# Sums of squares of the second token half in two views instead of four, their single-column products and the root's rows issued one token tile at a time between other products

## The chip, the cores and the metric

The kernel runs on one core of a Trainium2 chip, in one launch. The metric is the device time of the whole program in microseconds (us). Five engines work side by side, each in its own order, and wait for each other through semaphores: PE (TensorE, matrix products; its weight loads are listed apart as PEld), DVE (VectorE), ACT (ScalarE), POOL (GpSimd) and SP, which issues most DMAs. PE writes its results into PSUM banks, everything else works in SBUF.

## The reference

The reference is a trunk of two layers on 1024 tokens of 1024 values. Layer 0 has a forgetting softmax attention (FoX), layer 1 a gated linear attention (GLA); each is followed by a SwiGLU. Every sub-layer is preceded by an RMS norm that is scaled and shifted by a conditioning vector. Cut to what matters here:

```python
def rms_norm(x, g):
    y = xf * lax.rsqrt(jnp.mean(xf * xf, axis=-1, keepdims=True) + EPS)
    return (y * g).astype(x.dtype)

def modulate(h, shift, scale):
    return h * (1.0 + scale[:, None, :]) + shift[:, None, :]

for i in range(DEPTH):                      # DEPTH = 2
    sh1, sc1, g1, sh2, sc2, g2 = jnp.split(c_act @ ada_w[i] + ada_b[i], 6, axis=-1)
    h = modulate(rms_norm(x, norm1_g[i]), sh1, sc1)
    y = forgetting_attention(h, ...) if i == 0 else gated_linear_attention(h, ...)
    x = x + g1[:, None, :] * y
    h = modulate(rms_norm(x, norm2_g[i]), sh2, sc2)
    x = x + g2[:, None, :] * swiglu(h, ffn_w_in[i], ffn_w_out[i])
return rms_norm(x, final_g)
```

The change concerns three of the norms: the second norm of both layers (ahead of the SwiGLU) and the first norm of layer 1 (ahead of the GLA).

## The kernel before

**Layout.** x is held transposed: eight tiles `xs[k]` of 128 features by 1024 tokens, and all work goes over two halves of 512 tokens (`hf` 0 and 1). Each float32 product is made of three products of rounded parts (`mm3`, lines 240 to 243): high times high, high times low, low times high, accumulated in one PSUM bank. A tile of the output sums over k = 0 to 7, so it is 24 products of 512 columns. High parts are made by ACT, low parts (the remainder) by DVE or POOL.

**The end of a sub-layer.** `last_chunk` (line 1079) runs the output projection, for half 0 and then for half 1, over eight feature tiles m. After each, DVE adds the result to `xs[m]` (line 1074), and `SumSq` (lines 571 to 591) takes over: ACT squares the new tile into a view `v[m]` (line 583), and DVE or POOL adds views together (line 590), v0+v1, v2+v3 and so on, as a tree. For half 0 the whole tree is added, to a single view. For half 1 the tree stops early (`LATE1 = 7`): views 0 to 3 are added into view 0, view 5 into view 4, and views 6 and 7 are left alone. These four views, the roots, are what is handed on. At the very end of the program the squares are summed by another branch, which the change leaves alone.

**The norm.** `rms_cols` (line 526) sums over the features, which lie on the partitions: for each of the 4 token tiles and for each root, the view's 128 tokens are loaded as weights and multiplied by a column of ones, into one column of the PSUM tile `sp` (line 531). DVE scales the sums and adds EPS (line 534), POOL takes the power -1/2 (line 535). `rms_rows` (line 538) then spreads the root over the partitions: four products, one for each token tile, with the identity as the moving operand, fill the PSUM tile `rb` (line 543). Each of these float32 products appears in the trace as two instructions. Behind them DVE multiplies x by `rb` and the modulation, and ACT and DVE (or POOL) split the result into high and low parts: `normed` (line 1175) and `split_t` (lines 1182 and 1183) ahead of a SwiGLU, `norm_half` (lines 549 to 569) ahead of the GLA.

**Ahead of the SwiGLU.** `ffn` (line 1140) calls `rms_rows` for half 1 right after `last_chunk` (line 1199), then `second_half` (lines 1209 to 1220, called at line 1327), which norms and splits half 1 and makes the differences that a Strassen-like scheme needs. The first eight output tiles are plain ones (`plain_tile`, line 1330): three on half 0, then four on half 1, then one more on half 0. The first three give PE something to do while half 1 is normed. The order is tied at line 1352: in the second plain tile, products with k of 2 and more stand behind the last single-column product, and those with k of 6 and more behind the last row of `rb` (`GK = (2, 6)`); the third tile stands behind the rows too.

**Ahead of the GLA.** `norm_mixer` (line 1545) calls `norm_half` at the end of layer 0's SwiGLU, for either half. The GLA begins with value projections of half 0's tokens, `gv_body` (line 1611): 48 products of 256 columns each, for two pairs of token tiles. The first is free, the second is tied behind the single-column products (line 1848), and what follows, `a_body` and the rest, behind the rows of `rb` (line 1850).

**What sets the order.** The program is written in one sequence and a planner, which simulates the engines' time (`schedule_with_timeline_sim=True`), makes of it the order in which each engine gets its instructions. It may issue an instruction ahead of earlier written ones. `tc.issue_after(ins)` holds it to an order on one engine without a semaphore: what is traced within stands behind `ins` on the same engine. On the chip the engines keep the planned order.

## Time and profile before

| | us |
|---|---|
| three runs | 2414.92, 2417.11, 2417.97 |
| median of the runs | 2417.11 |
| profiled execution, from first to last instruction (span) | 2415.5 |
| PE busy | 2373.4 (98%) |
| DVE busy | 1672.9 (69%) |
| POOL busy | 1203.4 (50%) |
| ACT busy | 1191.8 (49%) |

The profiled execution is one of its own beside the three runs; no time is given for it but its span. Its mean granted PE clock over the span is 0.993 of full speed. Positions in the trace are counted from the span's start. The single-column products of the three norms stand at 662 to 672 us (SwiGLU of layer 0), 1313 to 1322 us (GLA) and 1751 to 1761 us (SwiGLU of layer 1). In rows of the timeline, neighbours of one kind are merged and their number stands behind an x; a busy time counts instructions in flight, so an engine can be busy without working at its peak. PSUM and SBUF tiles are named with their buffer numbers left out (`sp_b`, `rb_b`, `ss_s`); `p_b` is a SwiGLU tile's sum, `gv_b` one of the value projection, `o_s` a weight, `B` a normed input.

### The profile page before, as it was taken

The numbers are of one execution on the slowest core, as the hardware profiler recorded it, in microseconds if no ns is written. First come the engines' busy times: TensorE is split into PE (matmuls) and PEld (weight loads), VectorE is DVE, ScalarE is ACT, GpSimd is POOL, SyncE is SP. The second block draws the span as 40 slices with busy tenths as digits, with TensorE's granted clock in tenths as the row PEclk, the third lists the DMA queues.
The fourth block names the chain that finished last, engine by engine and source line by source line (L and its number), as shares of the span: only waits on it lengthen the run. The fifth ranks groups of instructions, "written<-read, shape, count | busy, mean of one in ns | idle before, by whom it ended". The sixth has DMA issues, their size and how long they took to land.

```text
span 2415.5 us, 36053 instructions
## 1 busy us (share of the span) xinstructions
PE 2373.4 (98%) x12342; PEld 2018.3 (84%) x12342; DVE 1672.9 (69%) x2789; ACT 1191.8 (49%) x2288; POOL 1203.4 (50%) x1071
## 2 busy tenths in 40 slices
PE   7999999999999999999999999999999999999998
PEld 6788888878888888888888888898888888888888
DVE  6577677676687877876787545435586767675787
ACT  4665555675544444445324856654343333345325
POOL 4343344432347878853263646662335656653262
PEclk9999999999999999999999999999999999999999
DMA  9233333123335555457665334434325444347664
GB/s 272 72 106 114 100 111 105 62 97 114 127 103 178 184 172 174 155 187 260 228 201 171 89 110 126 135 124 154 114 85 172 164 133 151 133 174 256 232 202 148
DMA packets 329359, 361.88 MB, mean 150 GB/s; under 512 B 24460, under 2 KB 252968, under 8 KB 329176
## 3 DMA queue, kind: packets, MB, share of 16 engines
q1 hardware_dynamic: 328984, 359.57, 45.4%
q8 instruction: 97, 1.59, 0.3%
q14 instruction: 86, 0.70, 0.1%
q10 hardware_dynamic: 192, 0.02, 0.0%
HBM read 269.25 MB, written 90.24 MB: 149 GB/s over the span
## 4 chain that ended last, share of the span: by engine, by line
PE 82%; DVE 5%; DMA 4%; ACT 3%; issue 2%; POOL 2%; SPq 1%; DVEq 0%; POOLq 0%; ACTq 0%
PE p_b L243 16%; PE p_b L241 16%; PE p_b L242 16%; PE o_b L979 2%; PE t_b L965 2%; PE qk_b L241 2%; PE qk_b L243 2%; PE qk_b L242 2%; PE s_b L934 1%; PE s_b L935 1%; PE gr_b L243 1%; PE gr_b L242 1%; PE gr_b L241 1%; PE vps_b L241 1%; PE vps_b L242 1%
## 5 line engine op out<-in xcount | busy, mean ns | idle before, releaser
L164 DVE TENSOR_TENSOR o_s<-xv_s,o_s 128x512 fp32r<-128x512 f32 (+1 forms) x376 | 341.4, 911 | 78.4 <-ACT o_s L163 77.5
L163 ACT CAST o_s<-xv_s 128x512 fp32r<-128x512 f32 (+1 forms) x376 | 217.8, 587 | 320.3 <-PE p_b L243 254.4
L242 PE MATMUL p_b<-B,o_s 128*128 128x512 f32 x608 | 238.1, 392 | 0.0
L243 PE MATMUL p_b<-B,o_s 128*128 128x512 f32 x608 | 237.7, 391 | 0.0
L241 PE MATMUL p_b<-B,o_s 128*128 128x512 f32 x608 | 236.2, 391 | 0.0
L945 POOL TENSOR_SCALAR lp_s<-lp_s,st 128x128 f32<-128x128 f32 (+7 forms) x128 | 98.1, 771 | 265.7 <-DVE st L944 214.7
L708 POOL TENSOR_TENSOR ex_s<-xv_s,xv_s 128x512 f32<-128x512 f32 (+1 forms) x64 | 89.1, 1393 | 261.5 <-DMA xv_s<-in_ffn_w_in_dram 97.1
L241 PE MATMUL p_b<-T,o_s 128*128 128x512 f32 x480 | 186.7, 389 | 0.0
L242 PE MATMUL p_b<-T,o_s 128*128 128x512 f32 x480 | 186.7, 389 | 0.0
L243 PE MATMUL p_b<-T,o_s 128*128 128x512 f32 x480 | 180.7, 389 | 0.0
L243 PEld LDWEIGHTS p_b<-B,o_s 128*128 128x128 f32 x608 | 114.7, 189 | 23.9
L241 PEld LDWEIGHTS p_b<-B,o_s 128*128 128x128 f32 x608 | 114.7, 189 | 23.8
L242 PEld LDWEIGHTS p_b<-B,o_s 128*128 128x128 f32 x608 | 114.7, 189 | 23.7
L943 ACT ACTIVATE lp_s<-lp_s,st 128x128 f32<-128x128 f32 (+7 forms) x128 | 99.3, 777 | 61.1 <-DVE st L939 58.7
L381 POOL TENSOR_TENSOR ad_s<-ad_s,ad_s 128x512 f32<-128x512 f32 x62 | 89.4, 1442 | 54.0 <-ACT ad_s L379 29.6
L163 ACT CAST pt_s<-t_b 128x512 fp32r<-128x512 f32 (+1 forms) x160 | 79.6, 547 | 73.5 <-PE t_b L965 72.8
L710 POOL TENSOR_TENSOR xv_s<-ex_s,xv_s 128x512 f32<-128x512 f32 (+1 forms) x64 | 84.9, 1327 | 57.3 <-DVE o_s L164 55.1
L1319 DVE TENSOR_TENSOR ex_s<-ex_s,p_b 128x512 f32<-128x512 f32 x140 | 94.0, 680 | 27.0 <-PE p_b L243 26.9
L164 DVE TENSOR_TENSOR pt_s<-t_b,pt_s 128x512 fp32r<-128x512 f32 (+1 forms) x160 | 96.8, 631 | 13.2 <-ACT pt_s L163 12.9
L243 PEld LDWEIGHTS p_b<-T,o_s 128*128 128x128 f32 x480 | 90.1, 188 | 18.7
L241 PEld LDWEIGHTS p_b<-T,o_s 128*128 128x128 f32 x480 | 90.1, 188 | 18.7
L242 PEld LDWEIGHTS p_b<-T,o_s 128*128 128x128 f32 x480 | 90.1, 188 | 18.7
(1952 smaller groups left out, 7505.7 us busy)
## 6 DMA issues: line engine op xcount, KB each, us to landing
xv_s<-in_ffn_w_in_dram SPq DMA_DIRECT2D x176, 256.0 KB, 3.0
hid_B<-x SPq DMA_DIRECT2D x70, 512.0 KB, 2.7
ad_s<-in_ada_w_dram SPq DMA_DIRECT2D x384, 64.0 KB, 1.9
hid_T<-x SPq DMA_DIRECT2D x36, 512.0 KB, 2.8
xv_s<-in_ffn_w_out_dram SPq DMA_DIRECT2D x96, 192.0 KB, 4.1
ada_s<-in_ada_w_dram SPq DMA_DIRECT2D x128, 128.0 KB, 2.6
xv_s<-in_ffn_w_out_dram SPq DMA_DIRECT2D x40, 256.0 KB, 2.8
T2o<-hid_T SPq DMA_DIRECT2D x18, 512.0 KB, 9.0
```

The costliest lines, as they stand in the source:

```text
L163: nc.scalar.copy(hi, src)
L164: nc.vector.tensor_sub(lo, src, hi.bitcast(F32))
L241: nc.tensor.matmul(ps, ah, bh, start=start, stop=False)
L242: nc.tensor.matmul(ps, ah, bl, start=False, stop=False)
L243: nc.tensor.matmul(ps, al, bh, start=False, stop=stop)
L381: nc.gpsimd.tensor_add(acc, acc, raw)
L708: nc.gpsimd.tensor_add(s1, a21, a22)
L710: nc.gpsimd.tensor_sub(a11, s1, a11)
L943: nc.scalar.activation(lp, lp, AF.Exp, bias=mcur, scale=-1.0, accum_out=st[:, qi, 2:3])
L945: nc.gpsimd.tensor_scalar(lp, lp, st[:, qi, 3:4], 1.0, op0=ALU.mult, op1=ALU.mult)
L965: nc.tensor.transpose(tp[:, i, :], lps[qi][:, psl(2 * b + jj)], ident)
L1319: nc.vector.tensor_add(d, d if src is None else dest(G, src), ps)
```

## The change

It has four parts.

- `SumSq` for half 1 adds on: after m = 5 DVE adds view 4 into view 0, and after m = 6 view 6 into view 0. The roots are now two, views 0 and 7.
- `mm3` issues its three products through a new function `product`. Where a queue `between` holds pieces of work, `product` takes one from it after each product, ties it behind that product, and ties the next product behind the piece.
- `rms_later` gives the norm as such pieces: the sums of one token tile (four pieces), the root (DVE and POOL), a number of empty pieces, and the rows of one token tile (four pieces). With the last row, what follows from it on the other engines is traced.
- The pieces go, ahead of the SwiGLU, between the products of the second plain tile from k = 2 on (8 empty pieces), and ahead of the GLA between the products of the second value projection (13 empty pieces). The old ties to the sums and rows are gone there, except that `a_body` and the rest of the GLA still stand behind the last row. `second_half` is now traced with the last row instead of ahead of the plain tiles, and the GLA's norm of half 1 within the second value projection.

```diff
+    between, tail = deque(), []
+
+    def product(ps, a, b, start, stop):
+
+        with ExitStack() as es:
+            if tail:
+                es.enter_context(tc.issue_after(tail.pop()))
+            nc.tensor.matmul(ps, a, b, start=start, stop=stop)
+        if between:
+            f = between.popleft()
+            with tc.issue_after(last_of("P")):
+                if f is not None:
+                    f()
+            tail.append(last_of("P"))
+
     def mm3(ps, ah, al, bh, bl, start, stop):
-        nc.tensor.matmul(ps, ah, bh, start=start, stop=False)
-        nc.tensor.matmul(ps, ah, bl, start=False, stop=False)
-        nc.tensor.matmul(ps, al, bh, start=False, stop=stop)
+        product(ps, ah, bh, start, False)
+        product(ps, ah, bl, False, False)
+        product(ps, al, bh, False, stop)
...
-    GK = (2, 6)
+    GK = 2
...
+    def rms_later(ss, nm, psr, then, gap=8):
+
+        at = {}
+
+        def sums(t):
+            if t == 0:
+                at["sp"] = psr([P, 4], F32, f"sp{nm}")
+            for i, q in enumerate(ss):
+                nc.tensor.matmul(at["sp"][:, t:t + 1], q[:, psl(t)], ones, start=i == 0, stop=i == len(ss) - 1)
+
+        def root():
+            rs = at["rs"] = sm.tile([P, 4], F32, tag="rs", name=f"rs{nm}")
+            nc.vector.tensor_scalar(rs, at["sp"], 1.0 / D, EPS, op0=ALU.mult, op1=ALU.add)
+            nc.gpsimd.tensor_tensor(rs, rs, mhalf[:, 0:4], op=ALU.pow)
+
+        def row(t):
+            if t == 0:
+                at["rb"] = psr([P, HALF], F32, f"rb{nm}")
+            nc.tensor.matmul(at["rb"][:, psl(t)], at["rs"][:, t:t + 1].to_broadcast([P, P]), ident,
+                             start=True, stop=True)
+            if t == 3:
+                rb_ins.append(last_of("P"))
+                then(at["rb"])
+
+        return ([lambda t=t: sums(t) for t in range(4)] + [root] + [None] * gap
+                + [lambda t=t: row(t) for t in range(4)])
...
     def norm_half(xs, ss, hs, l, hf, psr, tmp):
 
+        if hf:
+            second_norm.extend(rms_later(ss, f"{l}0{hf}", psr,
+                                         lambda rb: norm_views(rb, xs, hs, l, hf, tmp), 13))
+            return
...
-            self.roots = {0: [self.v[0]], 8: [self.v[0]], 7: [self.v[0], self.v[4], self.v[6], self.v[7]],
+            self.roots = {0: [self.v[0]], 8: [self.v[0]], 7: [self.v[0], self.v[7]],
...
+            if self.late == 7 and m in (5, 6):
+                nc.vector.tensor_add(v[0], v[0], v[4 if m == 5 else 6])
...
-        rb = rms_rows(ss1[0], f"{l}11", psr)
...
-        def second_half():
+        def second_half(rb):
...
-        second_half()
...
-                with ExitStack() as es:
-                    for k_, ins in after:
-                        if k >= k_:
-                            es.enter_context(tc.issue_after(ins))
-                    mm3(ps, w.hi[:, k % 4, :], w.lo[:, k % 4, :], hi(t), lo(t), k == 0, k == 7)
+                if k == GK:
+                    between.extend(small)
+                mm3(ps, w.hi[:, k % 4, :], w.lo[:, k % 4, :], hi(t), lo(t), k == 0, k == 7)
...
-        plain_tile(0, 1, 0, ((GK[0], sp_ins[-1]), (GK[1], rb_ins[-1])))
-        plain_tile(1, 0, 0, ((0, rb_ins[-1]),))
+        plain_tile(0, 1, 0, rms_later(ss1[0], f"{l}11", psr, second_half))
+        plain_tile(1, 0, 0)
...
-    with tc.issue_after(sp_ins[-1]):
-        vt.append(gv_body(0, wv, 1))
+    between.extend(second_norm)
+    vt.append(gv_body(0, wv, 1))
```

More of the change, by code (lines that the diff above doesn't have):

```diff
@@ L545, in rms_rows, with norm_views @@
         return rb
-    first_half = []
+    def rms_later(ss, nm, psr, then, gap=8):
[19 more added lines that the diff above has]
+                + [lambda t=t: row(t) for t in range(4)])
+    first_half, second_norm = [], []
     def norm_half(xs, ss, hs, l, hf, psr, tmp):
+        if hf:
+            second_norm.extend(rms_later(ss, f"{l}0{hf}", psr,
+                                         lambda rb: norm_views(rb, xs, hs, l, hf, tmp), 13))
+            return
         rb = rms_rows(ss, f"{l}0{hf}", psr)
         gates = [(SPM, sp_ins[-1]), (RBM, last_ins())]
+        norm_views(rb, xs, hs, l, hf, tmp)
+        first_half.append(last_of("G"))
+        return gates
+    def norm_views(rb, xs, hs, l, hf, tmp):
         cs = hsl(hf)
@@ L566, in norm_half @@
                 nc.gpsimd.tensor_sub(lo, y, hi.bitcast(F32))
-        if hf == 0:
-            first_half.append(last_of("G"))
-        return gates
     class SumSq:
@@ L1326, in ffn, with plain_tile @@
         gs = [Group(*g) for g in GROUPS]
-        second_half()
         wgs = [[[None, None], [None, None]] for _ in range(2)]
-        def plain_tile(kind, m, hf, after=()):
+        def plain_tile(kind, m, hf, small=()):
             wg = wgs[kind]
@@ L1351, in ffn @@
         plain_tile(0, 0, 0)
-        plain_tile(0, 1, 0, ((GK[0], sp_ins[-1]), (GK[1], rb_ins[-1])))
-        plain_tile(1, 0, 0, ((0, rb_ins[-1]),))
+        plain_tile(0, 1, 0, rms_later(ss1[0], f"{l}11", psr, second_half))
+        plain_tile(1, 0, 0)
+        assert not between
         for kind, m, hf in ((0, 0, 1), (0, 1, 1), (1, 0, 1), (1, 1, 1), (1, 1, 0)):
@@ L1847, in trunk @@
     vt = [gv_body(0, wv, 0)]
-    with tc.issue_after(sp_ins[-1]):
-        vt.append(gv_body(0, wv, 1))
+    between.extend(second_norm)
+    vt.append(gv_body(0, wv, 1))
+    assert not between
     with tc.issue_after(rb_ins[-1]):
```

## The prediction

> **What bounds the kernel now.** I read the page first: its span, its busy shares, and the chain of work that ended last.
>
> ```profile
> span 2415.5 us, 36053 instructions
> PE 2373.4 (98%) x12342; PEld 2018.3 (84%) x12342; DVE 1672.9 (69%) x2789; ACT 1191.8 (49%) x2288; POOL 1203.4 (50%) x1071
> PE 82%; DVE 5%; DMA 4%; ACT 3%; issue 2%; POOL 2%; SPq 1%; DVEq 0%; POOLq 0%; ACTq 0%
> ```
>
> TensorE sets the time: it is busy 98% of the span and carries 82% of the chain. Whatever it issues costs time, whatever it skips saves time, and work on the other engines is free until a product waits for it. The change touches three places: the norm of the second token half before the first SwiGLU (site 1, about 669 us), before the GLA mixer (site 2, about 1319 us), and before the second SwiGLU (site 3, about 1758 us). Next, TensorE's timeline at site 1. Columns: start, length, then the instruction; sp are the single-column sums of squares, rb the rows of the root, xN the merged instructions.
>
> ```profile
> 646.22 0.39 PE L243 MATMUL fo1421p_b<-ohh,wo_256l_s 128*128 128x512 f32 x1
> 646.45 0.95 PE L531 MATMUL sp_b<-ones,ss_s 128*128 128x1 f32 x8
> ...
> 649.89 0.39 PE L243 MATMUL fo1431p_b<-ohh,wo_256l_s 128*128 128x512 f32 x1
> 650.12 1.05 PE L543 MATMUL rb_b<-ident,rs 128*128 128x128 f32 x8
> 650.93 0.48 PE L241 MATMUL fo1441p_b<-ohh,wo_512h_s 128*128 128x512 f32 x1
> ...
> 661.93 0.62 PE L241 MATMUL p_b<-B,o_s 128*128 128x512 f32 x2
> 662.38 0.28 PE L531 MATMUL sp_b<-ones,ss_s 128*128 128x1 f32 x2
> ...
> 663.07 0.39 PE L241 MATMUL p_b<-B,o_s 128*128 128x512 f32 x1
> ...
> 668.75 0.39 PE L243 MATMUL p_b<-B,o_s 128*128 128x512 f32 x1
> 668.98 3.40 PE L531 MATMUL sp_b<-ones,ss_s 128*128 128x1 f32 x30
> 672.24 0.48 PE L241 MATMUL p_b<-B,o_s 128*128 128x512 f32 x1
> 672.55 0.40 PE L242 MATMUL p_b<-B,o_s 128*128 128x512 f32 x1
> ...
> 676.11 0.63 PE L243 MATMUL p_b<-B,o_s 128*128 128x512 f32 x1
> 676.53 1.19 PE L543 MATMUL rb_b<-ident,rs 128*128 128x128 f32 x8
> 677.48 0.48 PE L241 MATMUL p_b<-B,o_s 128*128 128x512 f32 x1
> ```
>
> Two things are to be seen. An undisturbed product takes 0.227 us (663.07 to 668.75 is 25 of them). And after the run of 30 single-column instructions the products become slow: rows grow from 0.39 to 0.63 us. The busy time by stretch, with the granted clock (the third number from the end), says why; the stretches are cut where the clock changes:
>
> ```profile
> 666.57:669.98 3.41, 3.41 (x22) 2.98 (x21) 1.31 (x3) 3.11 (x4) 2.63 (x2) 1.00 0.92 350
> 669.98:673.39 3.41, 3.41 (x27) 3.24 (x27) 0.16 (x1) 0.00 (x0) 1.12 (x2) 1.00 0.04 14
> 673.39:676.81 3.42, 3.42 (x11) 2.64 (x10) 0.00 (x0) 0.00 (x0) 0.29 (x1) 0.50 0.00 0
> 1321.93:1325.34 3.41, 3.41 (x18) 3.41 (x18) 0.16 (x1) 0.22 (x1) 1.02 (x1) 0.50 1.22 306
> 1762.24:1765.66 3.42, 3.42 (x10) 2.67 (x9) 0.00 (x0) 0.00 (x0) 0.34 (x1) 0.50 0.00 0
> 1393.60:1403.84 10.24, 9.75 (x35) 8.50 (x34) 4.64 (x9) 6.12 (x12) 6.58 (x7) 0.50 0.51 154
> ```
>
> At each of the three sites the clock falls to half for 3.41 us just after the single-column run, though TensorE counts as busy all through. The stretch that precedes the drop at site 1 (669.98 to 673.39) holds 2.26 us of single-column work and 1.15 us of products, 34%; the one before it, with 2.41 us of products, 71%, brought no drop.
>
> **The change part by part.**
>
> *Half the single-column products.* At each site, 4 token tiles times 4 views are 16 products, which the trace shows as 32 instructions (30 and 2 above). With two views they are 8 products, 16 instructions. Before: 668.75 to 672.55 holds two ordinary products and the 30, so 3.80 - 0.45 = 3.35 us; the early pair costs 661.93 to 663.07, 1.14 us less four products (0.91), 0.23 us. Together 3.58 us, 0.112 each. After, groups of four stand between products. Their price is not in the trace, but its neighbours are: a pair at 0.117 each, and eight at 0.119 each (646.22 to 649.89, 3.67 us, less 12 products, 2.72). It hardly depends on the grouping, so 16 x 0.119 = 1.90 us, and the saving is 1.7 us a site, **5.1 us** for three (bounds 4.9 and 5.4, by 0.12 and 0.112).
>
> *The rows of the root, likewise.* Still 8 instructions; eight together cost 649.89 to 650.93 less a product, 0.81 us. In four pairs at the pair's price it is 0.94. I take +0.1 a site, +0.3 in all (0 to 0.4).
>
> *The clock.* From 672.55 to 676.11 are ten products in 3.56 us, 1.29 too many; from 676.11 over the rows to 677.48 is 1.37 us against 1.04 for the same at 649.89 to 650.93. So one drop costs 1.6 us; three cost 4.8. In the new order four groups of 0.48 and four products of 0.227 last 2.83 us. The emptiest 3.41 us then hold 0.91 + 0.58 = 1.49 us of products, 44%. That lies between the 34% that dropped and the 71% that did not, and nearer to 34%, but with 0.34 us more of products than in the stretch that fell. I take no drop at sites 1 and 3 (bounds: none of the gain, or all of it).
>
> The page "TensorE: Matmul & The Clock Gate" of the Trainium skill (Part 1) says that the half clock follows an idle window of about 3.4 us and that the window runs free. Its length agrees with the 3.41 us here; "idle" does not, since the stretch that led to the drop held 1.15 us of products. By the page's rule alone no window here would be idle in the new order, and the gain would be the whole 4.8 us.
>
> The drops start at 673.39, 1321.93 and 1762.24 us: the distances are 190.0 and 319.0 times 3.4133 us. So the stretches stand on a fixed grid which has no tie to the work, and in other executions a run of 3.26 us will lie otherwise on it. If a drop needs the 2.26 us that preceded this one, it comes at (3.26 + 3.41 - 2 x 2.26) / 3.41 = 63% of the positions. The profiled execution had all three; the runs should have about two. I credit 0.65 x 1.6 = 1.0 us at each of sites 1 and 3.
>
> *The two added additions.* They run on DVE, whose cost is nothing as long as it has idle time, but the first group now waits for the last of them, and with it everything behind it on TensorE. DVE, ACT and POOL at site 1 and both engines at site 2:
>
> ```profile
> 662.81 0.63 ACT L583 ACTIVATE ss_s<-x 128x512 f32<-128x512 f32 x1 [2.62 <-DVE x L1074]
> 666.54 0.74 DVE L1074 SCALAR_TENSOR_TENSOR x<-fo1471p_b,modc,x 128x512 f32<-128x512 f32 x1
> 667.20 0.68 DVE L590 TENSOR_TENSOR ss_s<-ss_s 128x512 f32<-128x512 f32 x1
> 672.42 0.16 DVE L534 TENSOR_SCALAR rs<-sp_b 128x4 f32<-128x4 f32 x1 [4.54 <-PE sp_b L531]
> 672.66 1.02 POOL L535 TENSOR_TENSOR rs<-rs,mhalf 128x4 f32<-128x4 f32 x1 [2.29 <-DVE rs L534]
> 677.76 5.35 DVE L1175 SCALAR_TENSOR_TENSOR yb_s<-x,amul,rb_b 128x512 f32<-128x512 f32 x8 [5.18 <-PE rb_b L543]
> 683.04 2.57 DVE L1183 SCALAR_TENSOR_TENSOR B<-yb_s,modc,B 128x512 fp32r<-128x512 f32 x3
> ...
> 1317.96 0.67 DVE L590 TENSOR_TENSOR se_s<-se_s 128x512 f32<-128x512 f32 x1
> ```
>
> ```profile
> 1318.07 0.28 PE L243 MATMUL gv_b<-wv_4h_s,h1l 128*128 128x256 f32 x1
> 1318.68 3.63 PE L531 MATMUL sp_b<-ones,se_s 128*128 128x1 f32 x30 [0.33 <-DVE se_s L590]
> ...
> 1392.15 0.39 PE L241 MATMUL go_b<-gvt_s,ahl_s 128*128 128x256 f32 x1 [1.97 <-ACT ahl_s L163]
> ```
>
> At site 1 the present last addition ends at 667.88; in a queue such operations follow each other every 0.6 to 0.68 us, so two more end at about 669.1 to 669.2. TensorE comes to the first group at 668.98 - 0.23 (early pair gone) + 0.23 (one product) = 668.98. The wait is 0.2 us and something for a weight load that cannot be pulled ahead: **+0.3 us** each at sites 1 and 3 (bounds 0, if an addition is done before the last column of x, and 1.3, if both come after and are slowed). At site 2 DVE is already late: its addition ends at 1318.63 and TensorE starts 0.05 us later, 0.5 us after its last product should have let it. Two more additions put the start at 1319.9 if both come last, at 1318.7 if they are done before. I take the middle, **+0.7 us** more than now (bounds 0 and 1.3). A wait of 1.2 us and then 2.4 us of thin work (256-column products take half the time) is long enough to halve the clock at some positions of the grid, so of the clock's gain I credit site 2 with half as much, 0.5 us.
>
> *The root and what it feeds.* Between the last sum and the first row the present order needs 672.24 to 673.68 for DVE and POOL, 1.44 us. The new one leaves 10 products at site 1 (2.27 us) and 15 of 0.12 us at site 2 (1.8): covered. From the rows to the first product that needs the second half's weights there are now 30 products, 6.8 us; after the change one product of that tile and 24 of the next, 5.7 us. DVE's first remainder (L1183) is there 683.04 + 0.74 - 677.48 = 6.3 us after the rows. Three products on the high parts alone need no remainder (0.7 us), so it just holds; I put 0 and, if the planner sends a remainder first, 0.6 us a site. Nothing is moved past a DMA queue: the stores of x at both norms stay where they are written, and the added edges tie TensorE's instructions alone.
>
> *Sum.* On the profiled execution: -5.1 (columns) + 0.3 (rows) - 4.8 + 0.8 (clock, site 2 half kept) + 0.3 + 0.3 + 0.7 (waits) = -7.5 us, span 2408.0. The page gives no time for that execution beside its span of 2415.5 us; the runs' median is 1.6 us above it, and the lowest of the three 0.6 us below. For the runs, where the drops are not always there: -5.1 + 0.3 - 2.5 + 1.3 = -6.0, from the median of 2417.1 (2414.9 to 2418.0) to **2411.1 us**.
>
> **The rivals.**
>
> *The clock falls all the same* (0.15). Products between groups fill 44%, nearer to the 34% that fell. For it: TensorE counted as busy in both stretches, so the drop follows something finer than that. Against it: the share is higher by 0.34 us of products. Then -5.1 + 0.3 + 1.3 = -3.5, 2413.6 us.
>
> *The planner gives it back* (0.17). All engines' orders behind the sites are worked out anew. The trace has an example of what such an order can cost: 1.97 us of waiting at 1392.15, and the 10.24 us at half clock that follow. Where such a wait arises new, half of 10.24 us less what TensorE waited through, about 4, and 2 are lost: 6, which eats the gain, 2417 us. That the products go on without a gap at sites 1 and 3 speaks against it there. The same mechanism the other way (0.08), this wait gone: 2405 us.
>
> *The first group blocks TensorE* (0.10): the slower case. The trace shows an addition that the planner leaves lying: the square of 662.81 is ready at 663.44, its addition starts at 667.20, 3.8 us later, behind other work of DVE. If the last addition, whose square is ready at 667.35, is left as long, the first group starts after 671.8, 2.8 us late; TensorE is in order, so the tile behind it waits as well. An idle stretch of 2.8 us also halves the clock as before, and the waits pay nothing back: three sites cost 8.4, less 5.1, plus 0.3 and about one drop more than now, 1.6: +5.2, 2422 us. It decides from 1.6 us of wait a site. Against it: at site 1 DVE has nothing to do from 667.88 to 672.42, so an addition would have to be held by the planned order behind work that isn't there.
>
> **How the numbers follow.** The forecast has 0.50. About 0.2%, 4.8 us, is what runs of this kernel tell from no change. Below 2412.3 lie nine tenths of the forecast, the better order and a part of the clock case: 0.58. Within 4.8 us lie the rest of those and the order that gives it back: 0.31. Slower: 0.11, the blocked group and a little of the replanned order. The range goes from 2404 (the better order, and all bounds of the clock) to 2417 (the gain given back), and leaves out the blocked case and the last tenth.
>
> **What would show it.** At each site 16 single-column instructions instead of 32, in groups of four with one product between, each group 0.48 us; no stretch at 0.50 clock between the sums and the rows at sites 1 and 3; the products after them at 0.227 us; and the wait before the first group at 0.3, 1.2 and 0.3 us, with an addition on DVE as its releaser. Half clock after the groups shows the second step wrong; a wait over 1.6 us the third; sites that are 2 us shorter and an end that is not, that the order behind them took it.

## The result, and the profile after

The changed kernel is slower: a median of 2431.34 us (2430.13 to 2431.58) against 2415.62 us (2413.74 to 2417.97) for the kernel before on the same chip, a ratio of 1.0059 with a 95% interval of 1.0047 to 1.0072. The forecast was 2411.1 us with a range of 2404 to 2417. The time lies above the range, and the sign came out the other way.

The page's head, then TensorE's timeline at site 1 (start, length, instruction; in brackets the idle time ahead of it and what ended it). Line numbers have moved: products are L247, sums L570, rows L580.

```profile
span 2429.5 us, 35971 instructions
PE 2370.7 (98%) x12294; PEld 2014.3 (83%) x12294; DVE 1672.5 (69%) x2795; ACT 1192.8 (49%) x2288; POOL 1200.3 (49%) x1071
```

```profile
664.38 12.63 PE L247 MATMUL p_b<-B,o_s 128*128 128x512 f32 x55
676.85 0.50 PE L570 MATMUL sp_b<-ones,ss_s 128*128 128x1 f32 x4
...
678.89 0.50 PE L570 MATMUL sp_b<-ones,ss_s 128*128 128x1 f32 x4
679.25 2.56 PE L247 MATMUL p_b<-B,o_s 128*128 128x512 f32 x10
681.65 0.38 PE L580 MATMUL rb_b<-ident,rs 128*128 128x128 f32 x2
...
683.16 0.47 PE L247 MATMUL p_b<-B,o_s 128*128 128x512 f32 x1
685.00 0.98 PE L247 MATMUL p_b<-B,o_s 128*128 128x512 f32 x3 [1.36 <-ACT B L1233]
689.92 10.32 PE L247 MATMUL p_b<-B,o_s 128*128 128x512 f32 x35 [3.94 <-DVE B L1234]
```

The pieces stand as written: four groups of four single-column instructions, ten products, four pairs of rows. What is new stands around them. Ahead of the first group there are now 55 products; before there were 30, with the early pair between them. 24 of the 25 more are the third plain tile, whose products stood behind the rows. Behind the last row only one product is left, then three that need the high part of the second half, and then TensorE waits 3.94 us for DVE's first remainder. Of TensorE's waits in the whole run, those at the three sites (total, times, longest):

```profile
PE p_b L247 <- DVE B L1234: 7.9, 2, 4.0
...
PE sp_b L570 <- DVE se_s L642: 3.3, 1, 3.3
...
PE p_b L247 <- ACT B L1233: 2.7, 2, 1.4
```

Two sites wait 5.3 us each behind the rows, and site 2 waits 3.3 us ahead of its sums. The busy time by stretch shows what the clock does (columns: TensorE, weight loads, DVE, ACT, POOL, then the granted clock):

```profile
677.29:680.70 3.41, 3.41 (x22) 3.04 (x22) 0.68 (x2) 0.62 (x1) 1.02 (x1) 1.00 0.00 0
...
684.12:687.53 3.41, 0.98 (x3) 0.48 (x3) 3.41 (x7) 3.41 (x7) 3.19 (x3) 1.00 0.00 0
687.53:694.36 6.83, 4.44 (x11) 3.47 (x12) 6.83 (x11) 3.87 (x7) 1.79 (x2) 0.50 0.19 77
...
1329.24:1336.06 6.82, 6.82 (x33) 6.82 (x33) 0.16 (x1) 1.14 (x2) 1.02 (x1) 0.50 0.80 201
...
1783.21:1786.62 3.41, 0.00 (x0) 0.00 (x0) 3.41 (x5) 3.41 (x8) 3.10 (x3) 1.00 0.01 2
1786.62:1790.04 3.42, 3.12 (x7) 2.48 (x8) 3.42 (x7) 1.77 (x4) 0.00 (x0) 0.50 0.38 153
```

The sums and rows of sites 1 and 3 run at full clock now. The waits behind them halve it instead: for 6.8 us at site 1, 3.4 us at site 3. These rows give the loss of each site. Its measured length is the distance between two products that both kernels have, around the site:

| stage of the profiled execution | worked out, us | measured, us |
|---|---|---|
| site 1 | waits 3.94 + 1.36, half clock 4.44 / 2, less 1.86 for columns and 1.6 for the old drop: +4.1 | +4.6 |
| site 2 | wait 3.31 - 0.33, 3.41 us more at half clock (1.7), less 1.86 for columns: +2.8 | +2.6 |
| GLA, from its gate's first product to its last value product | | +1.5 |
| site 3 | waits 3.97 + 1.36, half clock 3.12 / 2, less 1.86 and 1.6: +3.4 | +4.0 |
| all else | | +1.3 |

The sum is 14.0 us, the difference of the spans. In "all else" 2.45 us arise ahead of site 1, where TensorE's order is the same in both kernels; 1.7 of them are a second stretch at half clock at 301.8 us, which e_lock below, whose time is shorter than that of the kernel before, has too.

At site 2 DVE and TensorE show why the sums wait:

```profile
1322.06 1.29 DVE L639 TENSOR_TENSOR se_s<-se_s 128x512 f32<-128x512 f32 x1
1323.27 2.35 DVE L164 TENSOR_TENSOR w2t<-w2raw_s,w2t 16x512 fp32r<-16x512 f32 x2
...
1326.27 1.41 DVE L642 TENSOR_TENSOR se_s<-se_s,se_s 128x512 f32<-128x512 f32 x2
...
1327.82 0.58 PE L570 MATMUL sp_b<-ones,se_s 128*128 128x1 f32 x4 [3.31 <-DVE se_s L642]
```

The planner puts splits of gate weights (L164) between the last addition of the old kind (L639) and the two added ones (L642).

### The profile page after: what moved, and what is told of

It is laid out like the page before. It is cut to its first block, busy times and chain, and to the rows that moved or that the text cites. A ratio compares the mean times of both kernels' runs of the same rounds, so it can differ in the third digit from the quotient of the medians.

```text
span 2429.5 us, 35971 instructions
## 1 busy us (share of the span) xinstructions
PE 2370.7 (98%) x12294; PEld 2014.3 (83%) x12294; DVE 1672.5 (69%) x2795; ACT 1192.8 (49%) x2288; POOL 1200.3 (49%) x1071
## 4 chain that ended last, share of the span: by engine, by line
PE 82%; DVE 6%; DMA 4%; ACT 3%; issue 2%; SPq 2%; POOL 1%; DVEq 0%; POOLq 0%; ACTq 0%
PE p_b L247 44%; PE qk_b L247 5%; PE vps_b L247 3%; PE gr_b L247 3%; PE gv_b L247 3%; PE o_b L1030 2%; PE t_b L1016 2%; PE s_b L985 1%; PE s_b L986 1%; PE gk_b L247 1%; PE go_b L247 1%; DVE o_s L164 1%; SPq L303 1%; DMA adas_s<-in_ada_w_dram 1%; SPq L376 1%
## 5 line engine op out<-in xcount | busy, mean ns | idle before, releaser
L247 PE MATMUL p_b<-B,o_s 128*128 128x512 f32 x1824 | 441.9, 392 | 10.6 <-DVE B L1234 7.9
L247 PEld LDWEIGHTS p_b<-B,o_s 128*128 128x128 f32 x1824 | 344.5, 189 | 83.2 <-DVE B L1234 8.8
L164 DVE TENSOR_TENSOR o_s<-xv_s,o_s 128x512 fp32r<-128x512 f32 (+1 forms) x376 | 341.7, 912 | 78.2 <-ACT o_s L163 77.5
L247 PE MATMUL p_b<-T,o_s 128*128 128x512 f32 x1440 | 345.6, 389 | 0.0
L247 PEld LDWEIGHTS p_b<-T,o_s 128*128 128x128 f32 x1440 | 270.4, 188 | 56.1
L759 POOL TENSOR_TENSOR ex_s<-xv_s,xv_s 128x512 f32<-128x512 f32 (+1 forms) x64 | 89.5, 1398 | 262.6 <-DMA xv_s<-in_ffn_w_in_dram 93.0
L164 DVE TENSOR_TENSOR pt_s<-t_b,pt_s 128x512 fp32r<-128x512 f32 (+1 forms) x160 | 96.9, 632 | 13.7 <-ACT pt_s L163 13.4
L990 DVE CUSTOM_DVE_ANT_0 lp_s<-s_b,cum_s 128x512 f32<-128x512 f32 (+3 forms) x128 | 72.8, 571 | 39.9 <-PE t_b L1016 20.9
L1030 PE MATMUL o_b<-pt_s,v_s 128*128 128x256 f32 x512 | 94.2, 294 | 5.9 <-DVE pt_s L164 3.3
L209 POOL TENSOR_TENSOR w_l_s<-w__s,w_h_s 128x256 fp32r<-128x256 f32 x120 | 89.7, 782 | 17.6 <-ACT w_h_s L206 17.6
L771 POOL TENSOR_TENSOR xv_s<-xv_s,xv_s 128x512 f32<-128x512 f32 x40 | 56.0, 1399 | 80.5 <-issue 60.2
L1544 DVE TENSOR_TENSOR x<-x,p_b 128x512 f32<-128x512 f32 x112 | 75.0, 681 | 27.6 <-PE p_b L247 23.2
L760 POOL TENSOR_TENSOR xv_s<-xv_s 128x512 f32<-128x512 f32 (+1 forms) x64 | 91.7, 1433 | 4.5
L247 PE MATMUL qk_b<-h0h,w_h_s 128*128 128x512 f32 x224 | 92.0, 411 | 0.0
L1231 DVE TENSOR_TENSOR x<-sg_s,x 128x512 fp32r<-128x512 f32 x58 | 66.4, 1145 | 36.0 <-ACT x L1230 34.7
```

The source lines that it names most:

```text
L164: nc.vector.tensor_sub(lo, src, hi.bitcast(F32))
L209: (nc.gpsimd if i < lo_p else nc.vector).tensor_sub(lo[:, cs], rw[:, cs], hi[:, cs].bitcast(F32))
L247: nc.tensor.matmul(ps, a, b, start=start, stop=stop)
L759: nc.gpsimd.tensor_add(s1, a21, a22)
L760: nc.gpsimd.tensor_sub(a21, a11, a21)
L1030: nc.tensor.matmul(ops, lv, pts[b][:, hl, 2 * jj:2 * jj + 2, :], start=j == 0 and hl == 0, stop=False)
```

## The experiments

All are edits of one of the two kernels, timed against the kernel before on the same chip. The third tile is "free" as in the changed kernel or "held" behind the last row as before; "views" is the number of roots that the single-column products read, two with the added additions and four without; "run" means that sites 1 and 3 issue them in one run, "pieces" token tile by token tile.

| kernel | tile | views | columns | us | ratio to before (95%) |
|---|---|---|---|---|---|
| before | held | 4 | run | 2415.6 to 2417.8 | 1 |
| changed | free | 2 | pieces | 2431.34 | 1.0059 (1.0047 to 1.0072) |
| e_tie3 | held | 2 | pieces | 2420.07 | 1.0015 (1.0005 to 1.0024) |
| e_untie | free | 4 | run | 2429.28 | 1.0056 (1.0043 to 1.0068) |
| e_half | half held | 2 | pieces | 2424.88 | 1.0032 (1.0020 to 1.0044) |
| e_roots | held | 2 | run | 2424.21 | 1.0037 (1.0024 to 1.0050) |
| e_four | free | 4 | pieces | 2436.29 | 1.0083 (1.0068 to 1.0099) |
| e_s2old | free | 2 | pieces, site 2 a run | 2431.05 | 1.0063 (1.0048 to 1.0078) |
| b1 | held | 2, one addition on POOL | pieces | 2422.39 | 1.0025 (1.0015 to 1.0036) |
| b2 | held | as b1, gate weights later | pieces | 2421.51 | 1.0021 (1.0012 to 1.0030) |
| e_lock | held | 2, POOL kept out | pieces | 2413.78 | 0.9984 (0.9975 to 0.9993) |
| e_four_tie | held | 4 | pieces | 2411.01 | 0.9978 (0.9969 to 0.9987) |
| e_four_tie_s2old | held | 4 | pieces, site 2 a run | 2419.82 | 1.0013 (1.0002 to 1.0024) |
| e_spread | held | 4 | pieces of half the size | 2419.73 | 1.0013 (1.0004 to 1.0022) |

The whole time does not say where an edit acts. The next table takes the profiled executions apart, between the same products as the table above (us longer than the kernel before). TensorE's part ahead of site 1 is 0.7 to 3.4 us longer in all of these executions and counts to "all else", which is not read here.

| kernel | site 1 | site 2 | GLA | site 3 | all else | in all |
|---|---|---|---|---|---|---|
| changed | +4.6 | +2.6 | +1.5 | +4.0 | +1.3 | +14.0 |
| e_untie | +4.8 | -1.1 | -1.3 | +6.4 | +3.2 | +12.0 |
| e_half | +1.4 | +2.7 | +1.3 | -0.1 | +2.2 | +7.5 |
| e_tie3 | +1.2 | +2.5 | -6.4 | +4.3 | +1.0 | +2.6 |
| e_lock | -2.1 | +1.0 | -3.4 | -2.1 | +0.6 | -6.0 |
| e_four_tie | -1.0 | -1.1 | -6.0 | +0.5 | -0.8 | -8.4 |
| e_spread | +2.4 | -2.6 | +1.7 | +2.4 | +0.5 | +4.4 |

**The place of the third tile.** e_tie3 holds it again, in an otherwise changed kernel:

```diff
-        plain_tile(1, 0, 0)
         assert not between
+        with tc.issue_after(rb_ins[-1]):
+            plain_tile(1, 0, 0)
```

> The changed kernel with one order put back: the third plain tile's products stand behind the last row again. Theory A (the order): without that order its 24 products were put ahead of the sums, and half 1's tiles had nothing left to cover the norm. Then sites 1 and 3 lose their wait of 1.4 and 3.9 us behind the rows and the half clock there; TensorE instead waits 2 to 2.5 us at the first group for the two additions (which ended at 673.7 us where it would arrive at 671.4), so each site ends about 1 us ahead of the kernel before instead of 4.6 us behind: 2431.3 - 2 x 5 = about 2421 us. Theory B (the additions): the sums are late because DVE is, and the order only filled the wait: each site gains at most the difference of 5 us of waits and 2.5 us, and the half clock stays: 2426 to 2429 us. Theory C (the groups between products cost by themselves): no gain, 2431 us.

It ran 11.3 us faster than the changed kernel, and the time is the one that theory A foretold, but by luck. Theory A had both sites gain, and only site 1 does (3.4 us); site 3 is no shorter than in the changed kernel. 7.9 us came in the GLA stage, whose code is the same in both, so the time of this run alone shows little about the tile. TensorE at site 1:

```profile
664.55 7.19 PE L247 MATMUL p_b<-B,o_s 128*128 128x512 f32 x31
674.03 0.58 PE L570 MATMUL sp_b<-ones,ss_s 128*128 128x1 f32 x4 [2.29 <-DVE ss_s L642]
...
676.50 4.12 PE L247 MATMUL p_b<-B,o_s 128*128 128x512 f32 x10
...
681.96 6.63 PE L247 MATMUL p_b<-B,o_s 128*128 128x512 f32 x28
688.81 3.47 PE L247 MATMUL p_b<-B,o_s 128*128 128x512 f32 x14 [0.22 <-DVE B L1234]
```

28 products behind the rows leave 0.22 us of the wait for DVE. But the sums, now 24 products earlier, wait 2.29 us, and the ten products behind them take 4.12 us in place of the 2.56 above: half clock. At site 3 the same wait is followed by 10.2 us at half clock, which eats the gain there. So the added additions do hold up the sums, and in the changed kernel the moved tile hides it. The reverse edit, e_untie, takes the hold out of the kernel before and changes nothing else:

```diff
-        plain_tile(1, 0, 0, ((0, rb_ins[-1]),))
+        plain_tile(1, 0, 0)
```

> The kernel before with one edit: the third plain tile's 24 products no longer have to stand behind the last row of the root. All 64 single-column products, one run of them, no added additions. In the planned order 15 of the 24 then stand ahead of the sums, 6 between sums and rows, and only 6 products in place of 30 are left between the rows and the first product of the second half. Theory A (the place of that tile is what costs): DVE's remainder is there about 6.3 us after the rows, 6 products cover 1.4 us and three high-part products 0.7, so TensorE waits about 3 to 4 us at each of sites 1 and 3 on the split of the second half, and the clock may halve once more there: 2423 to 2428 us. Rival B (the pieces cost, the place is harmless): 2415 to 2418, no wait behind the rows.

```profile
683.91 1.05 PE L543 MATMUL rb_b<-ident,rs 128*128 128x128 f32 x8
...
691.48 0.50 PE L242 MATMUL p_b<-B,o_s 128*128 128x512 f32 x1 [3.96 <-DVE B L1183]
```

That alone costs 13.7 us, nearly the 15.7 of the whole change, and 11.2 of the 12.0 us between the profiled executions lie at sites 1 and 3. e_half holds only the products with k of 4 and more, 12 of the 24:

```diff
+                with ExitStack() as es:
+                    if k >= held:
+                        es.enter_context(tc.issue_after(rb_ins[-1]))
...
-        plain_tile(1, 0, 0)
+        plain_tile(1, 0, 0, held=4)
```

> The changed kernel with the last 12 of the third plain tile's 24 products held behind the last row; the first 12 stay ahead of the sums. The planned order of the GLA stage is that of the changed kernel. Theory A (these products can cover either the late additions or DVE's split, and the loss is what neither covers): behind the rows there are 13 products in place of 1, so the waits of 3.9 and 1.4 us at each of sites 1 and 3 shrink by 12 x 0.227 = 2.7 us to about 2.5 in all; ahead of the sums there are 12 products more than in the kernel with the whole tile held, 2.7 us, so its wait of 2.3 us at the sums is gone or under 0.5. Then the time lies between: 2422 to 2427. Rival B (the wait behind the rows is tied to the additions and not to the number of products): it stays at 4 to 5 us, 2430.

```profile
673.62 0.50 PE L570 MATMUL sp_b<-ones,ss_s 128*128 128x1 f32 x4
...
679.93 3.91 PE L247 MATMUL p_b<-B,o_s 128*128 128x512 f32 x16
686.74 13.45 PE L247 MATMUL p_b<-B,o_s 128*128 128x512 f32 x51 [2.89 <-DVE B L1234]
```

Theory A foretold 2422 to 2427 us, and 2424.88 came. The wait at the sums is gone and the one behind the rows is 2.89 us, 2.4 less than 5.3 for 12 products, which last 2.7. Against the changed kernel sites 1 and 3 are 7.3 us shorter, and site 2 and the GLA stage are the same within 0.2 us, so here the place of the products alone makes the difference. The 24 products can cover either the additions ahead of the sums or DVE's split behind the rows.

**The added additions.** e_roots puts the two additions, and with them two views, into the kernel before, and leaves its order alone:

```diff
-            self.roots = {..., 7: [self.v[0], self.v[4], self.v[6], self.v[7]],
+            self.roots = {..., 7: [self.v[0], self.v[7]],
...
+            if self.late == 7 and m in (5, 6):
+                nc.vector.tensor_add(v[0], v[0], v[4 if m == 5 else 6])
```

> The kernel before with the two additions and two views alone: the sums stay in one run, of 16 instructions instead of 32, and all orders stay as they were. Theory A: the run is 1.7 us shorter at each site and too short to halve the clock (1.8 us of thin work in 3.4), against a wait for the additions of 1 to 2.5 us a site: 2408 to 2414 us. Theory B: the additions alone bring most of the loss: sums wait 3 us or more at each site, 2420 us and over. Theory C: faster by 5 us or more, since no group stands between products: 2406 to 2411 us.

```profile
PE sp_b L531 <- DVE ss_s L593: 5.0, 2, 2.5
PE sp_b L531 <- DVE se_s L593: 3.4, 1, 3.4
```

Waits of 2.5, 3.4 and 2.5 us at the sums, half clock for 6.8 us behind each, and 8.0 us lost. Half as many single-column instructions do not pay for it. e_four does the opposite in the changed kernel, that is, four views without the additions (the same lines reversed):

> The changed kernel without the two additions: four views as before, so that a group is eight instructions; the third plain tile stays free. Theory A: the third tile is still put ahead of the sums, the wait behind the rows stays at 4 to 5 us at sites 1 and 3, and 16 more instructions cost 1.7 us a site; site 2 loses its wait of 3.3 us: 2430 to 2434 us. Theory B: with the additions gone all waits go, sites 1 and 3 gain 5 us each and site 2 3 us, less 5 for the instructions: about 2423 us.

It was the slowest of all: the waits of 4.0 and 1.4 us behind the rows stay, there are 16 more instructions a site, and the clock halves twice at each of sites 1 and 3, once behind the longer thin stretch and once behind the wait. With the tile free, the additions are covered and their two views pay. e_s2old issues site 2 of the changed kernel in one run as before:

> The changed kernel with site 2 (the norm ahead of the GLA) issued as before, in one run behind the first value projection, but from two views. Sites 1 and 3 are as in the changed kernel. Both theories A and B leave their 8.6 us in place; site 2 was 2.6 us late at the first gate product and 1.5 us more by the end of the GLA. If the pieces made site 2's loss: 2427 us. If DVE's late additions made it, the sums wait as long as in the changed kernel (3.3 us) and the time stays at 2430 to 2432 us.

Its sums at site 2 still wait 3.5 us, so the additions and not the pieces make that loss.

**Why two additions of 0.6 us cost 2.3.** DVE and POOL at site 1 of the changed kernel:

```profile
669.65 0.68 DVE L639 TENSOR_TENSOR ss_s<-ss_s 128x512 f32<-128x512 f32 x1
670.37 3.36 DVE L642 TENSOR_TENSOR ss_s<-ss_s,ss_s 128x512 f32<-128x512 f32 x2
...
669.74 1.75 POOL L759 TENSOR_TENSOR ex_s<-xv_s,xv_s 128x512 f32<-128x512 f32 x1 [14.11 <-DMA xv_s<-in_ffn_w_in_dram]
671.57 1.62 POOL L760 TENSOR_TENSOR xv_s<-xv_s 128x512 f32<-128x512 f32 x1
```

L639 started just ahead of POOL's addition and took its 0.68 us. The next two started while POOL was at work, took 1.6 to 1.7 us each, and the second ended 0.54 us behind POOL's second, as if each had to wait for POOL's to end. b1 moved the first added addition, and the pair sum that it needs, to POOL:

```diff
-                (nc.gpsimd if d == 1 and m < 4 else nc.vector).tensor_add(...)
+                (nc.gpsimd if d == 1 and m < (6 if self.late == 7 else 4) else nc.vector).tensor_add(...)
...
-                nc.vector.tensor_add(v[0], v[0], v[4 if m == 5 else 6])
+                (nc.gpsimd if m == 5 else nc.vector).tensor_add(v[0], v[0], v[4 if m == 5 else 6])
```

> The changed kernel with the third plain tile held behind the last row, and the first of the two added additions (with the pair sum that it needs) on POOL, which is idle there, in place of DVE. Only one addition is then left behind the last square on DVE. Theory C (the 2.3 us of waiting at the sums of sites 1 and 3 is the two late additions on DVE): the wait falls to 0.3 to 1.2 us, the half clock that followed it comes less often, and the time falls from 2420.1 to 2414 to 2418. Rival D (the last addition is late by itself, behind POOL's additions and at their shared pace): the wait stays at 2 us or more and the time at 2419 to 2422. Site 2 still waits about 3 us in both.

```profile
665.18 2.27 POOL L639 TENSOR_TENSOR ss_s<-ss_s 128x512 f32<-128x512 f32 x1 [10.35 <-ACT ss_s L632]
667.52 1.62 POOL L642 TENSOR_TENSOR ss_s<-ss_s,ss_s 128x512 f32<-128x512 f32 x1
...
666.22 3.48 DVE L1234 SCALAR_TENSOR_TENSOR B<-ya_s,modc,B 128x512 fp32r<-128x512 f32 x2
...
671.18 1.56 DVE L642 TENSOR_TENSOR ss_s<-ss_s,ss_s 128x512 f32<-128x512 f32 x1 [0.17 <-ACT ss_s L632]
```

Theory C fell: the wait stayed at 2.1 us. POOL's additions now slowed DVE's remainders (1.78 us each in place of 0.7) ahead of the last two tiles of x, and the one addition left still took 1.56 us beside POOL's L760. b2 also held the gate weights' work on DVE behind the last addition at site 2:

```diff
-    w2t = big.tile([P, 2, 512], FR, tag=wslot, name="w2t")
+    with tc.issue_after(add_ins[-1]):
+        w2t = big.tile([P, 2, 512], FR, tag=wslot, name="w2t")
...
```

> As the one with the first added addition on POOL, and at site 2 the zeroing and splitting of the gate weights on DVE, which the planner had put ahead of the two added additions, is held behind the last of them. Theory C: the wait at the sums of site 2 falls from 3.0 to about 1 us and its half clock with it, 2 to 4 us less than without this: 2411 to 2416. Rival E: the weights that come later on DVE make the gate's products wait instead (aps or gk), so that the wait moves and the time stays within 1 us of the one without this edit.

The wait at site 2 was 3.8 us, against 4.6 in b1 and 3.0 in e_tie3, since POOL came to its additions only behind four splits of weights. It decided nothing but that this edit does not help. e_lock tests the shared pace directly. Its additions stay on DVE; POOL's two, and a third that comes later, are held behind the last of them by a POOL copy of one column of the sum:

```diff
+                if m == 6:
+                    mark = sm.tile([P, 1], F32, tag="mark", name="mark")
+                    nc.gpsimd.tensor_copy(mark, v[0][:, 0:1])
+                    add_ins.append(last_of("G"))
...
+            if add_ins:
+                es.enter_context(tc.issue_after(add_ins[-1]))
             nc.gpsimd.tensor_add(s1, a21, a22)
```

> The kernel with the third plain tile held behind the last row and the two added additions on DVE, with one edit: POOL's two 128x512 additions for the weights of the SwiGLU's first group, which ran beside DVE's added additions at sites 1 and 3, are held behind the last of them (a POOL copy of one column of the sum stands ahead of them). Theory F (DVE's two additions took 1.6 us each only since POOL held what both read through, and DVE waited for POOL's additions to end): they take 0.6 to 0.7 us each again, the wait at the sums of sites 1 and 3 falls from 2.3 to 0.3 to 0.6 us, and the clock's drop there comes less often or is shorter: 2414 to 2418 in place of 2420. Rival G (two dependent additions on DVE are slow in this place by themselves): they still take 1.6 us each, the wait stays over 2 us, 2420. Site 2 waits about 3 us in both.

```profile
670.20 1.49 DVE L642 TENSOR_TENSOR ss_s<-ss_s,ss_s 128x512 f32<-128x512 f32 x2
671.89 1.27 POOL L766 TENSOR_TENSOR ex_s<-xv_s,xv_s 128x512 f32<-128x512 f32 x1
671.83 0.58 PE L570 MATMUL sp_b<-ones,ss_s 128*128 128x1 f32 x4 [0.43 <-DVE ss_s L642]
...
674.31 2.56 PE L247 MATMUL p_b<-B,o_s 128*128 128x512 f32 x10
```

Theory F held: the two additions take 1.49 us together, the wait is 0.43 us at both sites, the ten products run at full clock (2.56 us), and the kernel is 4.0 us faster than the one before. Against e_tie3 the gain lies where the theory has it, 9.7 us at sites 1 and 3 of the profiled executions, while the GLA stage lost 3.0. The page "SBUF — State Buffer" of the Trainium skill ("Who interferes with whom") says that a DVE instruction with two SBUF inputs and a GpSimd instruction that reads SBUF exclude each other: the later one waits until the earlier has ended. The rows agree: the price falls on DVE's additions, which start second, 0.9 us each (1.63 against 0.75). Not all that DVE does beside POOL is slowed. Its updates of x read one tile from PSUM (DVE works on PSUM too, not in SBUF alone), and in b1 those at 669.62 and 670.28 us kept their 0.74 us while POOL's L759 ran from 669.11 to 670.85 us.

**What the pieces are worth.** e_four_tie is e_four with the tile held as in e_tie3, so that of the change only the pieces are left.

> The changed kernel with four views and no added additions (pieces of eight instructions between products), and with the third plain tile held behind the last row as before. It leaves only the pieces of the change. Theory A: the place of the tile and the late additions make the whole loss, so without both the time is that of before within 3 us (2413 to 2419), no wait over 0.5 us at the sums of sites 1 to 3 and none behind the rows. If four products between pieces of eight also keep the clock up, 2 to 5 us less: 2411 to 2414. Rival B: the pieces themselves cost (weight loads that change between a product and a single column, half clock for longer than before): 2420 or more with no wait to show for it.

```profile
669.86 0.72 PE L570 MATMUL sp_b<-ones,ss_s 128*128 128x1 f32 x6
...
684.60 11.63 PE L247 MATMUL p_b<-B,o_s 128*128 128x512 f32 x50 [0.24 <-DVE B L1232]
```

No wait over 0.3 us is left at the sites, and it has the shortest time of all. But its profiled execution is 8.4 us shorter than that of before, and only 1.6 of these lie at the three sites (-1.0, -1.1, +0.5). The GLA stage, whose code is the same, has 6.0. One row for the stage from before, e_tie3, e_four_tie and e_spread each:

```profile
1330.27:1603.61 273.34, 269.27 (x1648) 241.21 (x1647) 133.05 (x210) 178.69 (x371) 162.29 (x157) 0.98 0.38 115
```

```profile
1335.68:1602.57 266.89, 264.71 (x1648) 236.98 (x1647) 128.52 (x208) 177.02 (x368) 162.78 (x158) 1.00 0.42 117
```

```profile
1327.87:1595.25 267.38, 264.70 (x1647) 236.88 (x1646) 128.31 (x208) 179.65 (x371) 162.34 (x157) 1.00 0.41 118
```

```profile
1330.82:1605.90 275.08, 268.26 (x1648) 239.86 (x1646) 128.37 (x209) 179.68 (x371) 161.53 (x157) 0.99 0.40 115
```

The stage does the same work in 266.9 to 275.1 us. In the long ones, before's and e_spread's, TensorE waits 2.0 us for a split and 2.8 us for a masked copy, and the clock halves behind that. Two last kernels looked at this. e_four_tie_s2old issues site 2 in one run again:

> The four-view kernel with the third plain tile held, and site 2 issued in one run of single-column products as in the kernel before: pieces at sites 1 and 3 alone. Theory A (each site gains a little by its own pieces): between before and the kernel with pieces at all three sites, 2412 to 2415. Theory B (most of the gain is the other order of the GLA stage that follows the pieces of site 2, 6 of the 8.4 us between the profiled executions): 2414.5 to 2417 and the half clock near 1394 us is back.

e_spread cuts each piece in two:

```diff
-    GK = 2
+    GK = 1
...
-        def sums(t):
+        def sums(t, h):
...
+                if i // 2 == h:
                     nc.tensor.matmul(at["sp"][:, t:t + 1], q[:, psl(t)], ones, ...)
...
-        return ([lambda t=t: sums(t) for t in range(4)] + [root] + ...
+        return ([lambda t=t, h=h: sums(t, h) for t in range(4) for h in range(2)] + [root] + ...
```

> The four-view kernel with the third plain tile held, each token tile's eight single-column instructions in two pieces of four with a product between, and the first piece three products earlier at sites 1 and 3. A product of 0.227 us then stands by each 0.44 us of single columns, 34%, in place of 20%; the thin stretch grows from 4.0 to 5.1 us. Theory C (a stretch of 3.41 us needs more products than this to keep the clock): a drop at some sites as before, and a longer thin stretch brings it more surely: 2411 to 2414, not better. Theory D (the drops at sites 2 and 3 go): 2407 to 2410.

Both ended 2.6 to 2.7 us over before, and so beyond the ranges of both theories; the first comes nearer to theory B, and its clock halves at 1394 us again, as that theory said. Their GLA stages are 2.0 and 1.7 us longer than before's, 8 us longer than e_four_tie's. At the sites themselves e_spread lost 2.4 us at each of sites 1 and 3 (half clock for 6.8 us) and gained 2.6 at site 2. So a good part of e_four_tie's gain comes with its GLA order. Which edge in that stage makes the order turn out well was not tried and stays open.

## Why the prediction was wrong, point by point

**The step that failed** is in "The root and what it feeds": "after the change one product of that tile and 24 of the next, 5.7 us ... so it just holds; I put 0". I read the 24 products in the order in which the program writes them. The diff took away the hold that had kept them there, and the planner issued all of them ahead of the sums. Of the 25 products one was left. The cover that I had named was the right one, and so was the need: DVE's remainder is there 688.72 + 1.15 - 683.16 = 6.7 us behind the rows, against my 6.3. At sites 1 and 3 this makes 10.6 us of waits. What the hold is worth there is best read from e_untie, which drops nothing but the hold and is 11.2 us longer at these sites, and from e_half, which gives half of the tile back and is 7.3 us shorter there than the changed kernel. The 11.3 us of e_tie3 are near the same figure by chance, since 7.9 of them came in the GLA stage.

**The additions** were the second wrong term: +0.3, +0.7 and +0.3 us, with 1.3 as the upper bound at each. In the changed kernel sites 1 and 3 show no such wait, since the moved tile covers it. With the tile held it is 2.3 us, and 3.0 to 3.5 at site 2. The bound was too low since I priced two additions in a queue of DVE's own at 0.6 to 0.68 us each and did not ask what POOL ran at that moment. e_lock, with POOL out of the way, shows 0.43 us: the price I had given was right for an undisturbed DVE. At site 2 the planner, not the lock, sets most of the wait: other work on DVE stands ahead of the additions.

**The columns** were right: 676.85 to 679.25 is 2.40 us with three products (0.68), so 16 instructions cost 1.72, 0.107 each; the saving is 1.86 us a site where I had 1.7. **The rows** cost 681.65 to 683.16 less three products, 0.83 us; nothing in place of +0.1. **The root** is covered: POOL ends at 680.69, the first row starts at 681.65.

**The clock** came out as argued, and only where no wait spoils it: no half clock between sums and rows at sites 1 and 3 of the changed kernel, nor in e_half, e_s2old and e_lock. In e_tie3, b1 and b2, with the same pieces behind a wait of 2.1 to 2.3 us, it halves at both sites. My 44% was mis-sized: site 3 of the changed kernel has all four groups in one stretch, from 1772.97 us, and they leave 3.41 - 1.72 = 1.69 us for products, 50%. At 44% the step would have stood near the bound (see the last section). The drop is not gone with the one-run order for good; a wait ahead of the sums brings it back, and adds 1.6 us to the 2.3 at site 1 of e_tie3 (4.12 against 2.56 for the ten products). At site 2 I kept half of the drop; it grew from 3.41 to 6.83 us.

**The rivals.** The slower case was the first group blocking TensorE by 2.8 us a site. Its mechanism is real (2.3 to 3.5 us in e_tie3, e_roots and at site 2), but in the changed kernel it acts at site 2 alone, 2.6 of the 14.0 us between the profiled executions. The rival that made most of the loss, a transfer of cover from behind the rows to ahead of the sums, was not on my list, and its price stood in my own text: that same cover of 5.7 us, gone. The planner that "gives it back" elsewhere made +1.5 us in the GLA stage here, and up to 6.4 us the other way in other versions; I had taken the good case for the less likely of the two.

With the hold back and POOL out of the way, e_lock is 4.0 us faster than before. The forecast of 6.0 was for a kernel that kept the hold, but that the two are near is in part luck: of e_lock's 6.0 us between the profiled executions 3.4 lie in the GLA stage, where the forecast had nothing, and 3.2 at the three sites.

## What to carry to other kernels

When an edit removes an ordering edge, ask first what that edge kept back, and price the cover as if every product that becomes free had gone to the earliest place it can. A wait has to be looked for at both ends: products that no longer cover one wait may be hiding another. An addition on DVE is cheap only against what POOL runs at that moment, so read both engines' rows at the place where it will land. And price an edit stage by stage: in these kernels a stage with the same code differed by up to 8 us, as much as the effects in question.

## What the runs showed of the hardware

Two fp32 additions of 128x512 on DVE took 1.6 to 1.7 us each while POOL ran additions of the same size, and 0.75 each without them. POOL's own took 1.75 and 1.62 us with DVE's around and 1.27 without.

The half clock needs no idle time. Stretches of e_four_tie, in each of which TensorE counts as busy throughout, with pieces of eight single-column instructions and a product between:

```profile
671.99:675.41 3.42, 3.42 (x25) 3.12 (x24) 0.16 (x1) 0.00 (x0) 1.02 (x1) 1.00 0.02 5
...
1750.60:1754.01 3.41, 3.41 (x28) 3.27 (x28) 0.12 (x1) 0.00 (x0) 0.75 (x1) 1.00 0.09 35
1754.01:1757.43 3.42, 3.42 (x9) 2.65 (x8) 0.04 (x1) 0.00 (x0) 1.02 (x1) 0.50 0.00 0
```

The first holds the last 1.8 us of such a thin stretch and the clock stays; the second holds 3.1 us of one, and the clock halves. The four pieces last 4.0 us at either site. At site 1 a border of the stretches (671.99) falls into the middle of them, at site 3 it does not. The stretches have no tie to the work: the drops of this execution at 1320.52 and 1754.01 us are 127.0 times 3.4133 us apart (a third of 10.24 us), and 671.99 lies 190.0 such steps ahead of the first. The rule of the page "TensorE: Matmul & The Clock Gate" of the Trainium skill (Part 1), an idle window, fits the stretch of the changed kernel from 1783.21 us, which held no product at all, and not the one from 1750.60.

The runs narrow the bounds that the prediction had, 34% and 71% of a stretch in products. At 0.227 us a product, e_spread's stretch from 671.16 us holds five (33%) and e_four's from 676.28 us two and a run of 0.88 us (39%), and both were followed by half clock. In e_untie the run of single columns begins at 676.46 us, 1.38 us (40%) into its stretch, and the clock stayed, as it did with 50% at site 3 of the changed kernel. This is no rule for all stretches: the changed kernel's from 1779.80 us, with a wait of 1.36 us and only about a third in products, was not followed by half clock.
